# Recurrent mixer's head: transposed inputs and a first mix written tile by tile, in a fixed order on ScalarE and VectorE

## The chip, the cores and the metric

The kernel runs on one core of a Trainium2 chip. Its time is device microseconds of one execution. The engines are named as the profile names them: PE (TensorE, matmuls and transposes), ACT (ScalarE), DVE (VectorE), POOL (GpSimd) and SP (SyncE, which issues most DMAs).

## What is computed

A network of several layers in float32 on 256 tokens of width 1024. The change lies in one of them, the recurrent (RWKV) mixer of layer 2. Its reference, cut to what matters here:

```python
def rwkv7_time_mix(x, mu, w_rkv, w0, w1, w2, a0, a1, a2, g1, g2, ...):   # x is the normed input
    xx = jnp.pad(x, ((0, 0), (1, 0), (0, 0)))[:, :-1] - x        # previous token minus this one
    xr, xw, xk, xv, xa, xg = (x + xx * mu[i] for i in range(6))  # six mixes, indices 0 to 5
    r = xr @ w_rkv[0]
    k = xk @ w_rkv[1]
    v = xv @ w_rkv[2]
    w = -jax.nn.softplus(-(w0 + jnp.tanh(xw @ w1) @ w2)) - 0.5
    a = jax.nn.sigmoid((a0 + (xa @ a1) @ a2))
    g = jax.nn.sigmoid(xg @ g1) @ g2
    ...                                                          # then the recurrence over the tokens
```

The mixes have the indices r 0, w (the decay) 1, k 2, v 3, a 4, g 5.

## The kernel before

**Tiles.** The 256 tokens are two tiles of 128 (`TT`, t0 and t1). `h[t]` holds a tile's residual stream. A float32 product is made of three passes over numbers split into a high and a low part: `c.mm3` issues lines 116 to 118 (high weights by high input, low weights by high input, high weights by low input). So every input of a projection is wanted as a pair `xTh`, `xTl`, and every weight as `whi`, `wlo`, which ACT (line 81) and DVE (line 82) make from the loaded stage `st`.

**The head.** `c.rstd` takes the sum of squares of a tile on ACT (`junk`, line 128), and POOL makes the factor `rpre` of it. ACT scales the tile by it into `un`, in two halves (line 765); PE transposes each half in four blocks into `pt` (line 767); DVE multiplies by the norm's gain into `uT` (line 768), copies the token ahead of the tile into column 0 (line 771), and takes `xx` as one difference of 128x1024 (line 775).

**The mixes.** `shifted(i)` makes mix i for both tiles, in halves of 4 blocks: four times `xg` = `xx` by `mu[i]` on ACT (line 794, 128x128 each), plus `uT` on DVE (line 795), the high part on ACT (line 796), the low part on DVE (line 797). `proj(i, j, store)` calls it for its own index i and multiplies by `w_rkv[j]`; `lora(i, w, n)` does the same for a narrow weight. The calls stand in this order:

```python
    proj(2, 1, k)
    proj(0, 0, r)
    middle(0, 1, w1, AF.Tanh)      # calls lora(1, w1, 64)
    middle(1, 4, a1, AF.Copy)      # calls lora(4, a1, 64)
    gate_middle()                  # calls lora(5, g1, 160)
    ...
    part1(0)
    proj(3, 2, v)
    part2(0)
    part1(1)
```

`part1` makes the decayed keys and rates of one half of the heads (lines 865 to 928: `th`, `pb`, `E`, `kn`, `ar`, `bk`, `L`); `part2` inverts small blocks in a long chain of short DVE instructions on `Tc` (lines 940 to 945), which reads `comp`, a block that has gone to DRAM and back; `merges` (from line 957) follows.

**What sets the order.** A scheduler lays the instructions of the program on the five engines' queues by a simulated timeline; each queue then runs in its order, and waits are semaphores. So an edit at one place can move instructions that come much later.

Of the kernel before, what the change touches and what calls it, by code (L numbers as in the profile page):

```python
# [8 lines left out]
F32 = mybir.dt.float32  # L9
# [3 lines left out]
AF = mybir.ActivationFunctionType  # L13
# [3 lines left out]
D = 1024  # L17
# [634 lines left out]
def rwkv(c, pre, *args):  # L652
    with c.pool("rwkv") as mix, ExitStack() as phases:
        return rwkv_body(c, mix, pre, phases, *args)
# [58 lines left out]
def rwkv_body(c, mix, pre, phases, h, gpre, gpost, w_rkv, w0, w1, w2, a0, a1, a2, g1, g2, k_k, k_a, r_k, lnx_g,  # L713
              lnx_b, w_o):
    nc = c.nc
    HF = range(2)
    A = phases.enter_context(c.pool("rwkvA"))
    pad(A, 704)
    front = ExitStack()
    P1 = front.enter_context(c.pool("rwkvP"))  # L720
    close_A = phases.close
    open_B = lambda: phases.enter_context(c.pool("rwkvB"))
    TT = range(2)
    gb = c.load_bcast(gpost, "gb")
    muT, cum, mL, mK, mB, lowm, upm = pre.muT, pre.cum, pre.mL, pre.mK, pre.mB, pre.lowm, pre.upm
# [25 lines left out]
    def ring(shape, name):  # L751

        turn[0] ^= 1
        return c.wp.tile(shape, F32, name=name, tag="whi" if turn[0] else "wlo")

    ahead = {(1, 0): c.wblock(w_rkv[1], 0, 8, 0, 512)}

    uT, xx = [], []
    for t in TT:
        r = c.rstd(h[t], D, 1e-6, name="rpre")  # L760
        u = A.tile([128, 8, 129], F32, name=f"uT{t}")
        for q in range(2):
            pt = c.psT.tile([128, 4, 128], F32, name="pt", tag="pt")
            un = P1.tile([128, 512], F32, name="un", bufs=2)
            nc.scalar.activation(un, h[t][:, q * 512:q * 512 + 512], AF.Copy, scale=r)
            for k in range(4):
                nc.tensor.transpose(pt[:, k, :], un[:, k * 128:(k + 1) * 128], c.ident)
            nc.vector.tensor_mul(u[:, 4 * q:4 * q + 4, 1:], pt,
                                 gpre[:, 4 * q:4 * q + 4].unsqueeze(2).to_broadcast([128, 4, 128]))
        if t:  # L770
            nc.vector.tensor_copy(u[:, :, 0:1], uT[0][:, :, 128:129])
        else:
            nc.vector.memset(u[:, :, 0:1], 0.0)
        x = ring([128, 8, 128], f"xx{t}")
        nc.vector.tensor_sub(x, u[:, :, :128], u[:, :, 1:])
        uT.append(u)
        xx.append(x)

    nth = [0]

    def shifted(i):

        out = []
        for q in range(2):
            nth[0] += 1
            pool = P1 if i != 3 and nth[0] % 3 == 0 else c.act
            out.append([pool.tile([128, 4, 256], F32R, name="xT" + e, tag="xT" + e) for e in "hl"])
        for t in TT:
            s = slice(t * 128, t * 128 + 128)
            for q, (hi, lo) in enumerate(out):  # L790
                x = c.work.tile([128, 4, 128], F32, name="xg", tag="xg")
                for k in range(4):
                    kk = 4 * q + k
                    nc.scalar.activation(x[:, k], xx[t][:, kk], AF.Copy, scale=muT[:, kk, i:i + 1])
                nc.vector.tensor_add(x, x, uT[t][:, 4 * q:4 * q + 4, 1:])
                nc.scalar.copy(hi[:, :, s], x)
                nc.vector.tensor_sub(lo[:, :, s], x, hi[:, :, s])
        return out

    def lora(i, w, n):  # L800

        ws = c.wblock(w, 0, 8, 0, n)
        xs = shifted(i)
        G = c.psG.tile([128, 2, 256], F32, name="G", tag="G")
        m = lambda o, l, r, **kw: nc.tensor.matmul(o, l, r, skip_group_check=True, **kw)
        for e, c0 in enumerate(range(0, n, 128)):
            c1 = min(n, c0 + 128)
            o = G[:c1 - c0, e]
            for k in range(8):
                (wh, wl), (xh, xl) = ws(k), xs[k // 4]  # L810
                m(o, wh[:, c0:c1], xh[:, k % 4], start=(k == 0 and e == 0), stop=False)
                m(o, wl[:, c0:c1], xh[:, k % 4], start=False, stop=False)
                m(o, wh[:, c0:c1], xl[:, k % 4], start=False, stop=(k == 7 and c1 == n))
        return G
# [18 lines left out]
    r, k, v = {}, {}, {}  # L833

    def proj(i, j, store):
        xs = shifted(i)
        for q in HF:
            ws = ahead.pop((j, q), None) or c.wblock(w_rkv[j], 0, 8, q * 512, 512)
            for t in TT:
                G = c.psG.tile([128, 512], F32, name="G", tag="G")  # L840
                for kk in range(8):
                    xh, xl = (x[:, kk % 4, t * 128:t * 128 + 128] for x in xs[kk // 4])
                    c.mm3(G, xh, xl, *ws(kk), kk == 0, kk == 7)
                store[t, q] = S2(f"rkv{j}{t}{q}", f"rkv{j}", 4)
                nc.scalar.copy(store[t, q], G)  # L845
# [146 lines left out]
    def part3(q):  # L992
# [7 lines left out]
        for t in TT:  # L1000
# [91 lines left out]
            y[t, q] = yc  # L1092

    proj(2, 1, k)
    proj(0, 0, r)
    middle(0, 1, w1, AF.Tanh)
    middle(1, 4, a1, AF.Copy)
    gate_middle()
    front.close()
    phase[0] = phases.enter_context(c.pool("rwkvA2"))  # L1100
# [4 lines that stand above are left out]
# [738 lines left out]
```

## Time and profile before

| | us |
|---|---|
| median of 3 runs | 3363.42 |
| lowest and highest | 3344.17 and 3366.97 |
| the profiled execution | 3360.23 |
| its span in the trace | 3358.4 |
| busy: PE, DVE, ACT, POOL | 3185.8, 2342.0, 1595.5, 160.7 |
| mean granted clock of PE | 0.972 |

The span is the time from the first to the last instruction of one execution; the profiled execution's own time is 1.83 us longer. Busy times are sums over the whole span, so a stage in which PE waits is to be looked for in the windows and timelines. A matmul's end is modelled, so that durations of matmuls in a row overlap; the distance between their starts is the pace.

### The profile page before, as it was taken

How to read it: one execution, taken by the hardware profiler on the slowest of the kernel's cores; microseconds unless marked ns; L12 is line 12 of the kernel's file. 1: busy time of each engine (PE TensorE's matmuls, PEld its weight loads, DVE VectorE, ACT ScalarE, POOL GpSimd, SP SyncE). 2: the span in 40 equal slices, each digit the busy share in tenths (PEclk: the TensorE clock that was granted, in tenths of full speed). 3: DMA queues.
4: the chain of work that ended last, by engine and by line, in shares of the span. 5: the costliest groups of instructions: out<-in, count | busy, mean ns of one | idle time of the engine just before them, and what ended most of it. 6: DMA issues, size and time to landing. Idle time of an engine off the chain costs nothing. (4 is left out here: it accounts for less than half of the span.)

```text
span 3358.4 us, 45240 instructions
## 1 busy us (share of the span) xinstructions
PE 3185.8 (95%) x16491; PEld 2615.0 (78%) x16491; DVE 2342.0 (70%) x3767; ACT 1595.5 (48%) x2734; POOL 160.7 (5%) x248
## 2 busy tenths in 40 slices
PE   8999999989999987899999999999999999999898
PEld 7877887877887766787878877887778887775797
DVE  6767767777767766656777676765579877637787
ACT  5455454555445456224454465545544334424453
POOL 0001000000000001001010001010000000011000
PEclk9999999999999998889999999999999999998899
DMA  7663657643765753414656645631027554431463
GB/s 240 214 200 98 219 179 228 214 144 102 232 212 188 233 163 95 131 34 138 219 182 222 198 135 192 216 121 49 13 70 228 172 159 138 142 107 40 151 184 99
DMA packets 424667, 529.12 MB, mean 158 GB/s; under 512 B 54982, under 2 KB 342792, under 8 KB 424444
## 3 DMA queue, kind: packets, MB, share of 16 engines
q1 hardware_dynamic: 399548, 519.15, 49.4%
q10 hardware_dynamic: 24896, 7.08, 0.9%
q8 instruction: 130, 2.13, 0.3%
q14 instruction: 93, 0.76, 0.1%
HBM read 520.35 MB, written 5.78 MB: 157 GB/s over the span
## 5 line engine op out<-in xcount | busy, mean ns | idle before, releaser
L82 DVE TENSOR_TENSOR wlo<-st,whi 128x1024 fp32r<-128x1024 f32 (+1 forms) x810 | 974.4, 1215 | 406.6 <-ACT whi L81 370.2
L81 ACT CAST whi<-st 128x1024 fp32r<-128x1024 f32 (+1 forms) x810 | 835.7, 1044 | 533.5 <-PE po L118 173.1
L118 PE MATMUL G<-whi,xTl 128*128 128x512 f32 x1792 | 709.4, 396 | 19.2 <-DVE xTl L183 19.0
L116 PE MATMUL G<-whi,xTh 128*128 128x512 f32 x1792 | 714.6, 399 | 9.2 <-ACT rkv L845 2.2
L117 PE MATMUL G<-wlo,xTh 128*128 128x512 f32 x1792 | 705.9, 394 | 3.8 <-DVE wlo L79 3.8
L118 PEld LDWEIGHTS G<-whi,xTl 128*128 128x128 f32 x1792 | 338.8, 189 | 96.6 <-DVE xTl L183 27.0
L116 PEld LDWEIGHTS G<-whi,xTh 128*128 128x128 f32 x1792 | 339.3, 189 | 78.7 <-ACT whi L81 2.8
L117 PEld LDWEIGHTS G<-wlo,xTh 128*128 128x128 f32 x1792 | 339.3, 189 | 72.6 <-DVE wlo L79 5.7
L116 PE MATMUL po<-whi,hh 128*128 128x512 f32 x968 | 379.6, 392 | 9.1 <-ACT hh L260 7.2
L117 PE MATMUL po<-wlo,hh 128*128 128x512 f32 x968 | 377.6, 390 | 0.0
L118 PE MATMUL po<-whi,hl 128*128 128x512 f32 x968 | 339.9, 392 | 1.0 <-DVE hl L1743 0.5
L1707 PE MATMUL G<-xh,whi 128*128 128x256 f32 (+1 forms) x720 | 243.8, 339 | 8.4 <-ACT ub L1711 4.9
L1708 PE MATMUL G<-xl,whi 128*128 128x256 f32 (+1 forms) x720 | 242.1, 336 | 1.1 <-DVE xl L1232 1.1
L1709 PE MATMUL G<-xh,wlo 128*128 128x256 f32 (+1 forms) x720 | 241.5, 336 | 0.0
L251 ACT ACTIVATE sg<-G,rpre 128x256 f32<-128x256 f32 x176 | 83.8, 476 | 292.5 <-PE G L118 289.1
L116 PEld LDWEIGHTS po<-whi,hh 128*128 128x128 f32 x968 | 181.8, 188 | 50.6 <-ACT hh L260 10.9
L118 PEld LDWEIGHTS po<-whi,hl 128*128 128x128 f32 x968 | 180.5, 188 | 40.2 <-DVE hl L261 2.0
L1175 DVE SCALAR_TENSOR_TENSOR aa<-aw,sc,aa 128x1024 f32<-128x1024 f32 x140 | 174.9, 1282 | 51.5 <-DMA aw<-in_ada_w_dram 51.4
L117 PEld LDWEIGHTS po<-wlo,hh 128*128 128x128 f32 x968 | 181.8, 188 | 37.2
L1707 PEld LDWEIGHTS G<-xh,whi 128*128 128x128 f32 x720 | 138.8, 193 | 22.8 <-ACT ub L1711 5.3
L1708 PEld LDWEIGHTS G<-xl,whi 128*128 128x128 f32 x720 | 139.1, 193 | 15.4 <-DVE xl L1232 1.5
L1709 PEld LDWEIGHTS G<-xh,wlo 128*128 128x128 f32 x720 | 138.9, 193 | 14.3
(483 smaller groups left out, 4336.5 us busy)
## 6 DMA issues: line engine op xcount, KB each, us to landing
st<-in_ffn_w_in_dram SPq DMA_DIRECT2D x704, 256.0 KB, 4.1
st<-in_ffn_w_out_dram SPq DMA_DIRECT2D x242, 512.0 KB, 4.1
aw<-in_ada_w_dram SPq DMA_DIRECT2D x96, 512.0 KB, 4.7
st<-in_ffn_w_in_dram SPq DMA_DIRECT2D x88, 512.0 KB, 4.6
st<-in_swa_w_qkv_dram SPq DMA_DIRECT2D x24, 512.0 KB, 4.8
st<-in_gla_w_in_dram SPq DMA_DIRECT2D x24, 512.0 KB, 4.5
st<-in_rwkv_w_rkv_dram SPq DMA_DIRECT2D x24, 512.0 KB, 4.5
st<-in_na_w_qkv_dram SPq DMA_DIRECT2D x24, 512.0 KB, 4.1
```

Of the source, the lines that this page charges most:

```text
L81: nc.scalar.copy(hi, st)
L82: nc.vector.tensor_sub(lo, st, hi)
L116: m(out, xh, wh, start=start, stop=False)
L117: m(out, xh, wl, start=False, stop=False)
L118: return m(out, xl, wh, start=False, stop=stop)
L251: nc.scalar.activation(sg, G[:, :256], AF.Tanh, scale=rs[t][1])
L1175: nc.vector.scalar_tensor_tensor(acc[s], st, x, acc[s], op0=OP.mult, op1=OP.add)
L1707: m(Gf[:, a:b], wh, xh[:, k, a:b], start=(k == 0 and a == 0), stop=False, **kw)
L1708: m(Gf[:, a:b], wh, xl[:, k, a:b], start=False, stop=False, **kw)
L1709: m(Gf[:, a:b], wl, xh[:, k, a:b], start=False, stop=(k == 7 and b == ns * 256), **kw)
```

## The change

`shifted` is cut in two: `halves(i)` takes the buffers, `shift(i, t, out)` computes one tile's mix. The head is then one loop over the two tiles, inside a block in which ACT and DVE keep the written order of the block's own instructions (the scheduler may still set others between them). Per tile it is: sum of squares and `rpre`, column 0, both halves of `un`, then half by half the transposes, `uT`, and a difference `xx` of 128x512 (it was one of 128x1024 behind both halves); then `shift(1, t, mixed[1])` for the same tile. The mix so made is kept in `mixed` under the index 1, and `proj` asks `mixed` for its own index before it calls `shifted`.

```diff
-    uT, xx = [], []
-    for t in TT:
-        r = c.rstd(h[t], D, 1e-6, name="rpre")
...
-            un = P1.tile([128, 512], F32, name="un", bufs=2)
-            nc.scalar.activation(un, h[t][:, q * 512:q * 512 + 512], AF.Copy, scale=r)
...
-        x = ring([128, 8, 128], f"xx{t}")
-        nc.vector.tensor_sub(x, u[:, :, :128], u[:, :, 1:])
...
-    def shifted(i):
+    def halves(i):
...
+    def shift(i, t, out):
+        s = slice(t * 128, t * 128 + 128)
+        for q, (hi, lo) in enumerate(out):
+            x = c.work.tile([128, 4, 128], F32, name="xg", tag="xg")
+            for k in range(4):
+                kk = 4 * q + k
+                nc.scalar.activation(x[:, k], xx[t][:, kk], AF.Copy, scale=muT[:, kk, i:i + 1])
+            nc.vector.tensor_add(x, x, uT[t][:, 4 * q:4 * q + 4, 1:])
+            nc.scalar.copy(hi[:, :, s], x)
+            nc.vector.tensor_sub(lo[:, :, s], x, hi[:, :, s])
+
+    def shifted(i):
+        out = halves(i)
...
+    uT, xx = [], []
+    mixed = {1: halves(1)}
+    with c.tc.manual_schedule(engines={mybir.EngineType.Activation, mybir.EngineType.DVE}):
+        for t in TT:
+            r = c.rstd(h[t], D, 1e-6, name="rpre")
...
+            for q, un in enumerate(uns):
...
+                nc.vector.tensor_mul(u[:, z, 1:], pt, gpre[:, z].unsqueeze(2).to_broadcast([128, 4, 128]))
+                nc.vector.tensor_sub(x[:, z], u[:, z, :128], u[:, z, 1:])
+            uT.append(u)
+            xx.append(x)
+            shift(1, t, mixed[1])
...
     def proj(i, j, store):
-        xs = shifted(i)
+        xs = mixed.pop(i, None) or shifted(i)
```

The edit moves all later lines down by 13 (818 is the narrow product, 858 the copy of a projection, 880 and 957 are 867 and 944 of before). In the rows below a number behind a name tells one buffer from the next; `x4` is four instructions alike.

ACT at the head, from the second tile's sum of squares on, before:

```order
L128 ACTIVATE junk_11002,rprem_11001<-h1_91 128x1024
L794 ACTIVATE xg_11036<-xx0_10999,muT_10096 128x128 x4
L794 ACTIVATE xg_11044<-xx0_10999,muT_10096 128x128 x4
L765 ACTIVATE un_11009<-h1_91,rpre_11004 128x512
L765 ACTIVATE un_11017<-h1_91,rpre_11004 128x512
L796 CAST xTh_11032<-xg_11036 128x4x128
L796 CAST xTh_11034<-xg_11044 128x4x128
```

The same place now:

```order
L774 ACTIVATE xg_11008<-xx0_10993,muT_10096 128x128 x4
L776 CAST xTh_10975<-xg_11008 128x4x128
L774 ACTIVATE xg_11016<-xx0_10993,muT_10096 128x128 x4
L776 CAST xTh_10977<-xg_11016 128x4x128
L128 ACTIVATE junk_11025,rprem_11024<-h1_91 128x1024
L799 ACTIVATE un_11032<-h1_91,rpre_11027 128x512
L799 ACTIVATE un_11034<-h1_91,rpre_11027 128x512
L774 ACTIVATE xg_11051<-xx1_11036,muT_10096 128x128 x4
L776 CAST xTh_10975<-xg_11051 128x4x128
L774 ACTIVATE xg_11059<-xx1_11036,muT_10096 128x128 x4
L774 ACTIVATE xg_11077<-xx0_10993,muT_10096 128x128 x4
L776 CAST xTh_10977<-xg_11059 128x4x128
```

Both halves of the mix with index 1 (`xTh_10975`, `xTh_10977`) stand ahead of the second tile's sum of squares for t0 and behind its `un` for t1, and the first `xg` of the next mix (11077) comes behind them.

DVE behind the first tile's difference, before:

```order
L795 TENSOR_TENSOR xg_11036<-xg_11036,uT0_10981 128x512
L795 TENSOR_TENSOR xg_11044<-xg_11044,uT0_10981 128x512
L768 TENSOR_TENSOR uT1_11007<-pt_11008,gT_95 128x4x128
L797 TENSOR_TENSOR xTl_11033<-xg_11036,xTh_11032 128x4x128
L797 TENSOR_TENSOR xTl_11035<-xg_11044,xTh_11034 128x4x128
L768 TENSOR_TENSOR uT1_11007<-pt_11016,gT_95 128x4x128
L775 TENSOR_TENSOR xx1_11025<-uT1_11007 128x1024
L82 TENSOR_TENSOR wlo_11125<-st_11122,whi_11124 128x1024
L82 TENSOR_TENSOR wlo_11131<-st_11128,whi_11130 128x1024
L82 TENSOR_TENSOR wlo_11137<-st_11134,whi_11136 128x1024
```

And now, from the first half of the second tile's difference on:

```order
L808 TENSOR_TENSOR xx1_11036<-uT1_11030 128x512
L82 TENSOR_TENSOR wlo_11166<-st_11163,whi_11165 128x1024
L807 TENSOR_TENSOR uT1_11030<-pt_11044,gT_95 128x4x128
L82 TENSOR_TENSOR wlo_11172<-st_11169,whi_11171 128x1024
L82 TENSOR_TENSOR wlo_11178<-st_11175,whi_11177 128x1024
L808 TENSOR_TENSOR xx1_11036<-uT1_11030 128x512
L775 TENSOR_TENSOR xg_11051<-xg_11051,uT1_11030 128x512
L777 TENSOR_TENSOR xTl_10976<-xg_11051,xTh_10975 128x4x128
L775 TENSOR_TENSOR xg_11059<-xg_11059,uT1_11030 128x512
L775 TENSOR_TENSOR xg_11077<-xg_11077,uT0_10987 128x512
L777 TENSOR_TENSOR xTl_10978<-xg_11059,xTh_10977 128x4x128
L777 TENSOR_TENSOR xTl_11074<-xg_11077,xTh_11073 128x4x128
```

The second tile's difference is in halves with three `wlo` around the second transposed half, and the add into `xg_11077` stands behind both adds of the mix with index 1.

PE, the last transposes and the first products of the layer, before:

```order
L767 MATMUL pt_10990<-ident_85,un_10991 128x128 x4
L767 MATMUL pt_11008<-ident_85,un_11009 128x128 x4
L767 MATMUL pt_11016<-ident_85,un_11017 128x128 x4
L116 MATMUL G_11068<-whi_10953,xTh_11032 128x512
L117 MATMUL G_11068<-wlo_10954,xTh_11032 128x512
```

And now:

```order
L805 MATMUL pt_11001<-ident_85,un_10991 128x128 x4
L805 MATMUL pt_11037<-ident_85,un_11032 128x128 x4
L805 MATMUL pt_11044<-ident_85,un_11034 128x128 x4
L116 MATMUL G_11109<-whi_10953,xTh_11073 128x512
L117 MATMUL G_11109<-wlo_10954,xTh_11073 128x512
```

The order is the same; the product's inputs are now `xTh_11073` and `xTl_11074`, which stand on ACT and DVE behind the pairs 10975 to 10978 of the mix with index 1.

DVE late in the layer, where the last weight parts of the v projection (`wlo`, line 82) meet the chain of `part2(0)`, before:

```order
L82 TENSOR_TENSOR wlo_11940<-st_11937,whi_11939 128x1024
L904 TENSOR_TENSOR bo_12099<-rkv001_11363,km_12086 128x512
L902 SCALAR_TENSOR_TENSOR tha_12084<-tha_12084,kn_12089 128x512
L82 TENSOR_TENSOR wlo_11946<-st_11943,whi_11945 128x1024
L943 TENSOR_TENSOR pr_12005<-Tc_12003,comp_11646 128x1
L905 TENSOR_TENSOR bo_12099<-bo_12099,rkb_12060 128x512
L882 COPY em01_12080<-E1_12068 128x4
L944 TENSOR_REDUCE Tc_12003<-pr_12005 128x1
L907 TENSOR_REDUCE bon01_12102<-bo_12099 128x8
L943 TENSOR_TENSOR pr_12005<-Tc_12003,comp_11646 128x2x2
L944 TENSOR_REDUCE Tc_12003<-pr_12005 128x2
L943 TENSOR_TENSOR pr_12005<-Tc_12003,comp_11646 128x3x3
```

And now:

```order
L957 TENSOR_REDUCE Tc_12044<-pr_12046 128x3
L956 TENSOR_TENSOR pr_12046<-Tc_12044,comp_11687 128x4x4
L957 TENSOR_REDUCE Tc_12044<-pr_12046 128x4
L956 TENSOR_TENSOR pr_12046<-Tc_12044,comp_11687 128x5x5
L957 TENSOR_REDUCE Tc_12044<-pr_12046 128x5
L956 TENSOR_TENSOR pr_12046<-Tc_12044,comp_11687 128x6x6
L957 TENSOR_REDUCE Tc_12044<-pr_12046 128x6
L956 TENSOR_TENSOR pr_12046<-Tc_12044,comp_11687 128x7x7
L82 TENSOR_TENSOR wlo_11981<-st_11978,whi_11980 128x1024
L957 TENSOR_REDUCE Tc_12044<-pr_12046 128x7
L82 TENSOR_TENSOR wlo_11987<-st_11984,whi_11986 128x1024
L956 TENSOR_TENSOR pr_12046<-Tc_12044,comp_11687 128x8x8
```

The last two `wlo` of that projection (11940 and 11946) stood ahead of the chain's first step; they (11981 and 11987) now stand behind the product and the sum of its seventh step.

## Rows read from the trace of the kernel before

**Rows 1.** The page, part 1: busy us and share of each engine.

```profile
PE 3185.8 (95%) x16491; PEld 2615.0 (78%) x16491; DVE 2342.0 (70%) x3767; ACT 1595.5 (48%) x2734; POOL 160.7 (5%) x248
```

**Rows 2.** Windows of the recurrent layer: length, busy us per engine, clock, DMA.

```profile
1221.50:1234.40 12.90, 3.13 (x18) 2.50 (x17) 9.02 (x17) 11.48 (x23) 2.50 (x6) 0.64 0.45 123
1234.40:1238.60 4.20, 4.20 (x12) 3.13 (x11) 4.17 (x6) 0.83 (x3) 0.00 (x0) 0.50 0.00 0
1238.60:1276.50 37.90, 37.70 (x166) 30.74 (x165) 27.30 (x33) 29.85 (x65) 0.00 (x0) 1.00 0.60 183
1276.50:1310.00 33.50, 22.27 (x128) 18.00 (x126) 21.88 (x37) 26.90 (x75) 4.56 (x2) 0.85 0.05 18
1310.00:1382.50 72.50, 56.80 (x260) 43.73 (x260) 52.99 (x104) 18.93 (x33) 6.10 (x6) 0.78 0.51 145
```

**Rows 3.** PE's timeline at the head: start, duration, work, [idle before].

```profile
1224.16 1.46 PE L767 MATMUL pt<-ident,un 128*128 128x128 f32 x8 [2.61 <-ACT un L765]
1232.77 1.97 PE L767 MATMUL pt<-ident,un 128*128 128x128 f32 x8 [7.16 <-ACT un L765]
1234.39 0.78 PE L116 MATMUL G<-whi,xTh 128*128 128x512 f32 x1
...
1242.39 0.50 PE L116 MATMUL G<-whi,xTh 128*128 128x512 f32 x1 [0.20 <-ACT xTh L796]
```

**Rows 4.** Timeline of ACT over the same stretch.

```profile
1223.38 1.34 ACT L765 ACTIVATE un<-h,rpre 128x512 f32<-128x512 f32 x2 [0.41 <-POOL rpre L147]
1224.62 2.92 ACT L81 CAST whi<-st 128x1024 fp32r<-128x1024 f32 x3
1228.22 1.06 ACT L128 ACTIVATE junk<-h 128x1024 bf16<-128x1024 f32 x1 [0.67 <-DVE h L301]
...
1229.66 2.44 ACT L794 ACTIVATE xg<-xx,muT 128x128 f32<-128x128 f32 x8 [0.29 <-DVE xx L775]
1232.01 1.32 ACT L765 ACTIVATE un<-h,rpre 128x512 f32<-128x512 f32 x2
1233.23 1.12 ACT L796 CAST xTh<-xg 128x512 fp32r<-128x512 f32 x2
```

**Rows 5.** Timeline of DVE over the same stretch.

```profile
1228.41 1.22 DVE L775 TENSOR_TENSOR xx<-uT 128x1024 f32<-128x1024 f32 x1
...
1230.97 0.69 DVE L795 TENSOR_TENSOR xg<-xg,uT 128x512 f32<-128x512 f32 x1 [1.26 <-ACT xg L794]
...
1233.92 0.69 DVE L768 TENSOR_TENSOR uT<-pt,gT 128x512 f32<-128x512 f32 x1 [1.09 <-PE pt L767]
1234.53 1.28 DVE L797 TENSOR_TENSOR xTl<-xg,xTh 128x512 fp32r<-128x512 f32 x2
...
1237.59 3.49 DVE L82 TENSOR_TENSOR wlo<-st,whi 128x1024 fp32r<-128x1024 f32 x3
```

**Rows 6.** Timeline of POOL over the same stretch.

```profile
1229.83 0.57 POOL L147 TENSOR_TENSOR rpre<-rprem,mhalf 128x1 f32<-128x1 f32 x1
```

**Rows 7.** Line 794: all of them, and what ACT waited for.

```profile
L794 ACT ACTIVATE xg<-xx,muT x96: 384/388/404, 1229.7 to 1305.6; 128x128 f32<-128x128 f32 x96
...
  DVE xTl L797: 2.3, 4
```

**Rows 8.** Timelines late in the layer: ACT, then DVE, then PE.

```profile
1369.33 2.44 ACTq L742 DMA_DIRECT2D Ld<-L  x1
1371.82 0.60 ACT L867 ACTIVATE th<-z 128x512 f32<-128x512 f32 x1 [8.71 <-DMA g2b<-in_rwkv_g_dram]
...
1349.88 0.16 DVE L943 TENSOR_TENSOR pr<-Tc,comp 128x1 f32<-128x1 f32 x1 [1.78 <-DMA comp<-Ld]
...
1352.95 0.20 DVE L943 TENSOR_TENSOR pr<-Tc,comp 128x36 f32<-128x36 f32 x1
...
1373.02 2.06 PE L876 MATMUL pb<-cum,th 128*128 128x129 f32 x8 [5.47 <-DVE th L869]
...
1382.56 1.86 PE L957 MATMUL ps<-Z,L 128*128 128x128 f32 x7
```

More of the change, by code (lines that the diff above doesn't have):

```diff
@@ L756, in rwkv_body @@
     ahead = {(1, 0): c.wblock(w_rkv[1], 0, 8, 0, 512)}
-    uT, xx = [], []
-    for t in TT:
-        r = c.rstd(h[t], D, 1e-6, name="rpre")
-        u = A.tile([128, 8, 129], F32, name=f"uT{t}")
-        for q in range(2):
-            pt = c.psT.tile([128, 4, 128], F32, name="pt", tag="pt")
-            un = P1.tile([128, 512], F32, name="un", bufs=2)
-            nc.scalar.activation(un, h[t][:, q * 512:q * 512 + 512], AF.Copy, scale=r)
[L766 to L773, printed above, removed]
-        x = ring([128, 8, 128], f"xx{t}")
-        nc.vector.tensor_sub(x, u[:, :, :128], u[:, :, 1:])
-        uT.append(u)
-        xx.append(x)
     nth = [0]
-    def shifted(i):
+    def halves(i):
         out = []
@@ L787, in shifted @@
             out.append([pool.tile([128, 4, 256], F32R, name="xT" + e, tag="xT" + e) for e in "hl"])
-        for t in TT:
-            s = slice(t * 128, t * 128 + 128)
-            for q, (hi, lo) in enumerate(out):
-                x = c.work.tile([128, 4, 128], F32, name="xg", tag="xg")
-                for k in range(4):
[L793 to L797, printed above, removed]
@@ L798, in shifted @@
-        return out
+        return out
+    def shift(i, t, out):
[8 more added lines that the diff above has]
+            nc.vector.tensor_sub(lo[:, :, s], x, hi[:, :, s])
@@ new lines, in shifted @@
+    def shifted(i):
+        out = halves(i)
+        for t in TT:
+            shift(i, t, out)
+        return out
+    uT, xx = [], []
[3 more added lines that the diff above has]
+            r = c.rstd(h[t], D, 1e-6, name="rpre")
+            u = A.tile([128, 8, 129], F32, name=f"uT{t}")
+            if t:
+                nc.vector.tensor_copy(u[:, :, 0:1], uT[0][:, :, 128:129])
+            else:
+                nc.vector.memset(u[:, :, 0:1], 0.0)
+            uns = []
+            for q in range(2):
+                un = P1.tile([128, 512], F32, name="un", bufs=2)
+                nc.scalar.activation(un, h[t][:, q * 512:q * 512 + 512], AF.Copy, scale=r)
+                uns.append(un)
+            x = ring([128, 8, 128], f"xx{t}")
+            for q, un in enumerate(uns):
+                pt = c.psT.tile([128, 4, 128], F32, name="pt", tag="pt")
+                for k in range(4):
+                    nc.tensor.transpose(pt[:, k, :], un[:, k * 128:(k + 1) * 128], c.ident)
+                z = slice(4 * q, 4 * q + 4)
+                nc.vector.tensor_mul(u[:, z, 1:], pt, gpre[:, z].unsqueeze(2).to_broadcast([128, 4, 128]))
[3 more added lines that the diff above has]
+            shift(1, t, mixed[1])
```

## The prediction

> **What bounds the kernel now.** I read the page's engine shares first: PE is busy for 95% of the span [rows 1], so an edit pays only where PE stands still. The windows of this layer come next. While the head runs, PE works 3.13 of 12.90 us and ACT 11.48 [rows 2]; in the projections behind it PE is full (37.70 of 37.90 us); then come two stages in which PE idles again (22.27 of 33.50 and 56.80 of 72.50 us). The head's timelines say what ends the 12.90 us. PE's first product starts at 1234.39, behind the transposes of tile t1 at 1232.77, which had waited 7.16 us for ACT's `un` [rows 3]. ACT runs `un` of t0, three weight casts to 1227.54, t1's sum of squares, the eight `xg` of t0 at 1229.66 and `un` of t1 at 1232.01, then the two casts that the first product needs [rows 4]. DVE is always a step behind or ahead of that [rows 5]. So the head is one serial path through ACT, DVE and PE, and whatever is put into it shifts a stretch in which PE has no slack.
>
> **What the change does, read from the code.** It makes a first mix in the head and keeps it under index 1, the decay. `proj` asks for its own index, and its calls are 2, 0 and 3; index 1 is wanted only by `lora`, which calls `shifted(1)` and never asks. So nobody reads the new mix. The order shows it: PE's first product reads `xTh_11073` and `xTl_11074`, which belong to the mix of index 2, and the pairs 10975 to 10978 have no reader. The change therefore adds a whole mix to the serial path: 16 `xg` and 4 casts on ACT, 4 adds and 4 subtractions on DVE. That is 16 x 0.293 (the pace of eight `xg` in 2.44 us, one lasting 0.388 [rows 4, 7]) + 4 x 0.51 (the pace of two casts in 1.12) = 6.7 us of ACT and 8 x 0.59 (the pace of two in 1.28 [rows 5]) = 4.7 us of DVE.
>
> **The head, step by step.** I replay the queues of the order with the durations of the rows, on the clock of the trace before; nothing changes up to the casts that end at 1227.54.
>
> - t0. In halves, the first difference stands one DVE slot of 0.59 earlier than the whole one at 1228.41, so it runs 1227.82 to 1228.51, and `xg` starts at 1228.54 instead of 1229.66. The unread mix then runs step by step, since ACT's cast waits for DVE's add: four `xg` to 1229.81 (3 x 0.293 + 0.388), add to 1230.55, cast to 1231.2; the second half's `xg` to 1232.36, add to 1233.09, cast to 1233.74.
> - Only then comes t1's sum of squares, at 1233.63. From it to `rpre` it took 2.18 us (1228.22 to 1230.40 [rows 4, 6]), so `un` of t1 starts at 1235.84 instead of 1232.01: 3.8 us later. From `un` to `uT` it took 1.91 (1232.01 to 1233.92 [rows 4, 5]): 1237.75.
> - t1's differences. Between the first `uT` and the second half of `xx` stand, on DVE, one half of `xx`, another `uT` and three `wlo` of 1.14 each (3.49 for three): 3 x 0.60 + 3 x 1.14 = 5.2 us, so that the last half of `xx` starts at 1243.0 and ends at 1243.7. The unread mix's add for t1 stands behind it by the written order, though its `xg` is done at 1240.5; ACT stands for nearly 4 us. Add to 1244.35, cast to 1245.0, the second half's `xg` to 1246.1.
> - The mix that is read. Four `xg` to 1247.3, add to 1248.05, cast to 1248.7, and there the first product starts: **14.3 us later** than 1234.39. The wait of 0.20 inside the projections [rows 3] goes, since the weights' parts are long made: 14.1.
>
> Bounds: the unread work cannot cost less than ACT's 6.7 us less the 1.42 that ACT idles in that window [rows 2], so 5.3; add four hand-overs between ACT and DVE at up to 0.4 more than I allow, and it is 16. The transposes gain nothing; their cover is gone anyway, since PE is idle on both sides of them. [...]
>
> The halving of `xx` has a small price of its own. By the rows two halves at a pace of 0.59 to 0.60 take 0.07 to 0.1 us more than one of 1.22 [rows 5]. [...]
>
> **Behind the head.** In the projections and the narrow products every engine's work is the same and keeps its neighbours, so it shifts as a whole. Two places are re-ordered by the scheduler. In front of `part1(0)` the gate's activation now stands ahead of `th`, on which PE waits: 1 us, between 0 and 2. Late, the last two `wlo` of the v projection stand behind the seventh step of the chain on `Tc`. That chain starts when `comp` lands (1349.88) and was at its sixth step at 1352.95 [rows 8]; so the weights come some 7 us after PE could use them, of which about 2 are won back because PE starts that stretch earlier: 5 us, all of which I pass on to the merges at 1382.56 [rows 8]. The bounds are 0, if the later wait of PE for `th` (5.47) takes it up, and 12: the last copy of v and an `E` now stand on ACT behind the DMA issues of `part2(0)`, and such a queue held `th` for 8.71 us there [rows 8]. What follows the layer is re-ordered a little, at nothing or up to 2 us either way.
>
> Sum: 14.1 + 1 + 5 = 20 us. On the profiled execution's 3360.23 that is 3380.3; the median of the runs before is 3.2 higher, which would give 3383.5. I take **3382**.
>
> **The rivals.**
>
> 1. *The mix does what the edit says, or hides.* If the unread work could be passed over, only t1's late `un` would stay: the first product at about 1238.2, +3.8, and 3366 with the rest of the sum not spent. Against it: ACT is busy 11.48 of 12.90 us in that window [rows 2]. ACT would have to run a ready `xg` of the read mix ahead of a waiting cast; where `th` waited 8.71 us, it did so behind the queue's DMA issues [rows 8]. [...] A toolchain that drops writes nobody reads would give about the same time. 6 in 100.
> 2. *The late re-ordering costs nothing.* PE's wait for `th` takes it up: 3360.2 + 15 = 3375, some 3378 by the median. 16 in 100.
> 3. *Faster after all.* In the two stages behind the projections PE idles 11.23 and 15.70 us [rows 2]. With PE 14 us late, weights, mixes and DMAs are further ahead of it, and those waits could shrink. The price: to win, they must give back over 20 of 26.9 us, and the time would be about 3355. It decides whether they wait for stock or for a chain. Only 2.3 us of ACT's waits for `xTl` are of the first kind [rows 7]; the 5.47 us before `pb` end with DVE's `th`, which follows ACT and PE of the same stage [rows 8]. 4 in 100 for any gain, 2 for one of over 1%.
> 4. *Clearly slower.* The chain's wait for `comp` and the DMA issues on ACT add up: +12 at the second place instead of +5, with the head at its upper bound: 3360.2 + 16 + 2 + 12 = 3390, 3393 by the median; a further slip of t1's `th` by a queue like the 8.71 us puts it at 3400. It decides whether the last `wlo` are late by more than the 10 us or so that the merges are away. 14 in 100, some 9 of them beyond 1%.
>
> **How the numbers follow.** The forecast has 60 in 100: 3374 to 3390. About 1%, 33.6 us, is what a measurement of this kernel can tell from no change (three runs before lie within 22.8 us), so the forecast, a loss of 0.6%, falls within it. The range takes in rival 2 and the better part of rivals 1 and 4: 3360 to 3401. Faster by over 1%: 0.02; within 1%: 0.88; slower by over 1%: 0.10.
>
> **What would show it.** In the trace of the changed kernel: 112 `xg` instead of 96; PE's idle time ahead of the first product some 14 us longer, ended by the cast of line 776, with t1's transposes near 1236.6; ACT standing about 4 us ahead of a cast at 1244; the window of the projections as long as before; and PE waiting some 7 us in the v projection for `wlo` of line 82. I am wrong if the first product starts before 1240 (rival 1), or if the head is as replayed but the merges start less than 10 us later (rivals 2 and 3) or more than 28 (rival 4).

## The result

The changed kernel took 3389.84 us (median of six runs, 3380.38 to 3411.25), the kernel before 3353.42 in the same comparison (six runs, among them the three of the table ahead of the prediction): a ratio of 1.0106, with an interval of 1.0084 to 1.0128. Timed a second time (run e5 below) it was 1.0070, 1.0047 to 1.0094. It is slower by 20 to 36 us; the forecast was 20, and 3382. The profiled execution took 3385.51 us with a span of 3383.7.

The page's engine shares (busy us, share, instructions), against [rows 1], show 20 more instructions on ACT and 10 more on DVE; PE has as many as before and is busy 15.8 us longer. The group of line 774 shows where most of ACT's come from, 16 more `xg` than the 96 of before [rows 7]; the other four are casts:

```profile
PE 3201.6 (95%) x16491; PEld 2620.5 (77%) x16491; DVE 2343.8 (69%) x3777; ACT 1605.4 (47%) x2754; POOL 154.7 (5%) x248
```

and, in the group's row:

```profile
L774 ACT ACTIVATE xg<-xx,muT x112: 384/387/404, 1231.4 to 1324.4; 128x128 f32<-128x128 f32 x112
```

The windows of the stages (length, busy us with instruction counts, granted clock, DMA; cut where PE's starts lie, so that they do not fall on the borders of [rows 2]): the head has grown from 13.23 to 28.19 us between PE's starts, and PE works 4.12 us in it; the projections behind it are full as before.

```profile
1223.40:1251.60 28.20, 4.12 (x18) 2.70 (x16) 19.41 (x31) 17.48 (x41) 2.44 (x6) 0.56 0.39 112
1251.60:1298.10 46.50, 46.47 (x192) 38.10 (x193) 28.62 (x37) 35.76 (x80) 0.00 (x0) 0.93 0.41 126
1298.10:1324.00 25.90, 18.64 (x102) 15.39 (x100) 16.15 (x27) 21.07 (x60) 0.00 (x0) 0.80 0.01 4
1324.00:1406.10 82.10, 62.22 (x268) 46.60 (x268) 57.47 (x111) 21.88 (x42) 8.70 (x8) 0.74 0.47 128
```

PE's timeline at the head, against [rows 3] (start, duration, work, idle time before it and what ended it): the transposes of t1 wait 11.27 us instead of 7.16, and behind them PE stands for another 10.23, ended by the cast of the first mix that anybody reads.

```profile
1226.44 1.73 PE L805 MATMUL pt<-ident,un 128*128 128x128 f32 x8 [2.61 <-ACT un L799]
1239.43 1.97 PE L805 MATMUL pt<-ident,un 128*128 128x128 f32 x8 [11.27 <-ACT un L799]
1251.63 0.79 PE L116 MATMUL G<-whi,xTh 128*128 128x512 f32 x1 [10.23 <-ACT xTh L776]
```

ACT's timeline, against [rows 4]. The first two `xg` groups, with the casts behind them, are the unread mix of t0. Only then come t1's sum of squares (1236.52) and `un` (1238.66). The unread `xg` of t1 (1242.04) is followed by 3.93 us in which ACT stands.

```profile
1225.67 1.33 ACT L799 ACTIVATE un<-h,rpre 128x512 f32<-128x512 f32 x2 [0.42 <-POOL rpre L147]
...
1231.40 1.28 ACT L774 ACTIVATE xg<-xx,muT 128x128 f32<-128x128 f32 x4 [1.57 <-DVE xx L808]
1233.44 0.62 ACT L776 CAST xTh<-xg 128x512 fp32r<-128x512 f32 x1 [0.76 <-DVE xg L775]
1233.96 1.27 ACT L774 ACTIVATE xg<-xx,muT 128x128 f32<-128x128 f32 x4
...
1236.52 1.05 ACT L128 ACTIVATE junk<-h 128x1024 bf16<-128x1024 f32 x1
...
1238.66 1.33 ACT L799 ACTIVATE un<-h,rpre 128x512 f32<-128x512 f32 x2 [0.99 <-POOL rpre L147]
1242.04 1.28 ACT L774 ACTIVATE xg<-xx,muT 128x128 f32<-128x128 f32 x4 [2.05 <-DVE xx L808]
1247.24 0.62 ACT L776 CAST xTh<-xg 128x512 fp32r<-128x512 f32 x1 [3.93 <-DVE xg L775]
...
1250.96 0.62 ACT L776 CAST xTh<-xg 128x512 fp32r<-128x512 f32 x1 [0.25 <-DVE xg L775]
```

DVE over the same stretch, against [rows 5], shows what it stands for: the second half of t1's difference (line 808, 1245.92) comes behind the three `wlo`, two of them in one row here, and the add that ACT waits for (line 775) behind that. `kab` at the top waits 0.53 us for its own load, and the first difference behind it.

```profile
1230.34 0.43 DVE L872 TENSOR_SCALAR kab<-kab 128x512 f32<-128x512 f32 x1 [0.53 <-DMA kab<-in_rwkv_k_a_dram]
1230.68 0.69 DVE L808 TENSOR_TENSOR xx<-uT 128x512 f32<-128x512 f32 x1
...
1243.65 2.35 DVE L82 TENSOR_TENSOR wlo<-st,whi 128x1024 fp32r<-128x1024 f32 x2
1245.92 0.68 DVE L808 TENSOR_TENSOR xx<-uT 128x512 f32<-128x512 f32 x1
1246.52 0.68 DVE L775 TENSOR_TENSOR xg<-xg,uT 128x512 f32<-128x512 f32 x1
```

### The profile page after: what moved, and what is told of

Same layout as the page of the kernel before. It is cut to its first block, busy times and chain, and to the rows that moved or that the text cites. A ratio compares the mean times of both kernels' runs of the same rounds, so it can differ in the third digit from the quotient of the medians.

```text
span 3383.7 us, 45274 instructions
## 1 busy us (share of the span) xinstructions
PE 3201.6 (95%) x16491; PEld 2620.5 (77%) x16491; DVE 2343.8 (69%) x3777; ACT 1605.4 (47%) x2754; POOL 154.7 (5%) x248
```

## The experiments

All times of stages are distances between starts in PE's timeline of each profiled run: from the last product of the layer before to the first product of this one ("head"), to the first narrow product, to the first `pb`, to the first merge. Ratios are to the kernel before, timed beside each.

| run | head | to narrow | to pb | to merges | sum | ratio (interval) |
|---|---|---|---|---|---|---|
| before | 13.23 | 46.26 | 21.83 | 80.08 | 161.4 | |
| changed | 28.19 | 46.50 | 25.87 | 82.11 | 182.7 | 1.0106 (1.0084 to 1.0128) |
| e5 changed again | 27.58 | 45.22 | 24.63 | 84.97 | 182.4 | 1.0070 (1.0047 to 1.0094) |
| e1 no first mix | 12.56 | 46.33 | 21.74 | 84.17 | 164.8 | 1.0011 (0.9994 to 1.0029) |
| e2 index 2 | 10.47 | 57.98 | 21.79 | 86.48 | 176.7 | 1.0027 (1.0010 to 1.0044) |
| e3 unread mix in before | 25.06 | 46.56 | 25.56 | 77.06 | 174.2 | 1.0028 (1.0013 to 1.0043) |
| e4 interleaved | 10.84 | 49.99 | 20.49 | 79.39 | 160.7 | 1.0007 (0.9989 to 1.0025) |
| e6 rotation kept | 28.02 | 46.47 | 23.71 | 84.18 | 182.4 | 1.0053 (1.0031 to 1.0075) |
| e7 unread mix later | 12.23 | 54.97 | 21.69 | 84.42 | 173.3 | 1.0035 (1.0019 to 1.0052) |
| e8 interleaved, held | 10.23 | 50.57 | 22.25 | 76.83 | 159.9 | 1.0004 (0.9987 to 1.0022) |
| e9 late order back | 28.23 | 45.43 | 24.68 | 75.22 | 173.6 | 1.0056 (1.0036 to 1.0077) |
| e10 no written order | 23.99 | 45.49 | 24.71 | 81.19 | 175.4 | 1.0078 (1.0060 to 1.0095) |
| e11 halves only | 12.84 | 47.17 | 22.48 | 78.10 | 160.6 | 0.9978 (0.9963 to 0.9993) |
| e12 the same again | 12.96 | 45.79 | 23.29 | 78.34 | 160.4 | 1.0001 (0.9982 to 1.0020) |

**e1: the changed kernel without the first mix.**

```diff
-    mixed = {1: halves(1)}
+    mixed = {}
...
-            shift(1, t, mixed[1])
```

> The changed kernel without the first mix in the head; the halves of the differences and the written order stay. Theory (the unread mix is the cost): from the last product of the layer before to the first product of this layer 13 us within 1.5, as before (13.2) and not 28.2 as in the changed kernel; the late re-ordering of the weights stays, so the time is 0 to 6 us over the kernel before, ratio 1.000 to 1.003. Rival (the written order is the cost): over 20 us there, ratio 1.006 or more.

Head 12.56, ratio 1.0011: halves and written order together, without the mix, cost nothing there, they even gain 0.7 us. The late stretch is longer though (84.17 against 80.08), as the order said it would be. PE's timeline of this run, the last transposes (behind them the products follow at once):

```profile
1232.74 1.97 PE L805 MATMUL pt<-ident,un 128*128 128x128 f32 x8 [6.67 <-ACT un L799]
1234.36 0.78 PE L116 MATMUL G<-whi,xTh 128*128 128x512 f32 x1
```

**e2: the mix kept under the index that is asked for.**

```diff
-    mixed = {1: halves(1)}
+    mixed = {2: halves(2)}
...
-            shift(1, t, mixed[1])
+            shift(2, t, mixed[2])
```

> The changed kernel with the mix kept under index 2, which the first projection asks for, so that it is read. Theory: ACT does the same work up to the casts of tile t0, but PE now wants them: the first product comes about 10 us behind the last one of the layer before (3 us sooner than in the kernel before), and t1's products, behind its transposes, about 1 us later than before; ratio to before 0.998 to 1.004. Rival (the written order, which puts the second tile behind the first tile's mix, is the cost): as slow as the changed kernel, 1.008 or more.

The first product comes 10.47 us behind the last one, as the replay of this order said, but the ratio is still 1.0027, and the layer 15.3 us longer. The scheduler now puts t1's transposes behind the 24 products of t0, and PE's timeline shows the price, a wait of 6.93 us for t1's mix:

```profile
1233.10 0.79 PE L116 MATMUL G<-whi,xTh 128*128 128x512 f32 x1 [5.50 <-ACT xTh L776]
...
1241.56 1.03 PE L805 MATMUL pt<-ident,un 128*128 128x128 f32 x8
1249.53 0.80 PE L116 MATMUL G<-whi,xTh 128*128 128x512 f32 x1 [6.93 <-ACT xTh L776]
```

I had expected t1's products one us late; they came 5.7 us late (26.90 us behind the last product of the layer before instead of 21.23), since the place of the transposes and the three `wlo` in front of t1's second half were left out of that sum.

**e3: the kernel before with an unread mix.**

```diff
     def proj(i, j, store):
+        if i == 2:
+            shifted(1)
         xs = shifted(i)
```

> The kernel before with one extra mix of index 1 that nobody reads, ahead of the first projection's own; no written order, whole differences. It adds work and leaves nothing out. Theory: the first product about 24.5 us behind the last one of the layer before (11.5 more than before, since t1's scaled input isn't held up), and some 4 us more in the narrow products, whose buffers rotate otherwise; the late weights keep their place; ratio 1.004 to 1.006. Rival (written order): 13 us and ratio 1.000 to 1.002.

The head grew by 11.83 us with no written order at all, forecast 11.5. So the extra work alone is most of the cost; what the changed kernel has beyond it, 2.5 to 3.1 us in the head, e10 takes apart. PE's timeline of it:

```profile
1240.58 1.97 PE L767 MATMUL pt<-ident,un 128*128 128x128 f32 x8 [7.25 <-ACT un L765]
1253.91 0.80 PE L116 MATMUL G<-whi,xTh 128*128 128x512 f32 x1 [11.35 <-ACT xTh L796]
```

ACT's timeline says why 6.7 us of ACT's work cost 11.8. The first two rows are the kernel before, t1's part of the mix that is read: ACT waits 3.41 us for t1's `xx` and 1.49 for the add that stands behind three `wlo` on DVE, but PE has t0's products meanwhile. The other two are e3: the unread mix has the same two waits, and now they stand in front of PE's first product. 6.7 of work and 4.9 of waits make 11.6.

```profile
1237.77 2.45 ACT L794 ACTIVATE xg<-xx,muT 128x128 f32<-128x128 f32 x8 [3.41 <-DVE xx L775]
1241.72 0.62 ACT L796 CAST xTh<-xg 128x512 fp32r<-128x512 f32 x1 [1.49 <-DVE xg L795]
...
1245.58 2.45 ACT L794 ACTIVATE xg<-xx,muT 128x128 f32<-128x128 f32 x8 [3.41 <-DVE xx L775]
1249.53 1.22 ACT L796 CAST xTh<-xg 128x512 fp32r<-128x512 f32 x2 [1.50 <-DVE xg L795]
```

**e4: both tiles interleaved.** Index 2, and the second half of the block in this order (`scaled` makes the two `un`; `turned` does the transposes, `uT` and the difference of a half):

```diff
+        shift_half(2, 0, 0, *mixed[2][0])
+        uns = scaled(1, r)
+        shift_half(2, 0, 1, *mixed[2][1])
+        for q, un in enumerate(uns):
+            turned(1, q, un)
+            shift_half(2, 1, q, *mixed[2][q])
```

> Index 2, and the second tile's sum of squares and scaled input written between the halves of the first tile's mix, so that neither tile waits for the whole of the other. Theory: first product 9 to 11 us behind the last one of the layer before, t1's products 1 to 3 us sooner than in the kernel before, nothing moved in the late stage: 0 to 5 us under the kernel before, ratio 0.998 to 1.000. Rival (written order costs by itself): over the kernel before by 0.3% or more.

Head 10.84, but the projections take 3.7 us more, and the time can't be told from before (1.0007).

**e5: the changed kernel again.**

> The changed kernel once more, as a control, since the first comparison had six runs a side. If the layer is what the change costs, the stretch from the last product of the layer before to the merges is again 21 us longer than before (182.7 against 161.4), and the ratio 1.006 to 1.008, below the first 1.011; if the change also slows stretches outside the layer, 1.010 or more.

182.4 against 182.7: the layer's loss repeats within 0.3 us, though the stages in it differ by up to 2.9 us, while the ratio fell from 1.0106 to 1.0070, into the range that the layer explains.

**e6: the buffers of the later mixes as before.**

```diff
     mixed = {1: halves(1)}
+    nth[0] = 0
```

> The changed kernel with the counter that rotates the mixes' buffers set back behind the unread mix, so that the later mixes lie in the pools of before. Head unchanged: 28.2 us to the first product. Theory A (the narrow products' extra 4 us come of the rotation): 22 to 23 us from the first narrow product to the first pb, as before (21.8). Theory B (they come of an order that the scheduler moved: the second waT activation ahead of a cast that PE wants; the order still has it here): 24 to 26, the activation of the gate being back behind th.

23.71 us to `pb`, between what the two theories gave, so this run doesn't settle it: the gate's activation went back behind `th` with the buffers, and 1 to 2 of the 3 to 4 us with it, while PE's wait of 2.24 us in front of the third group of narrow products stayed as in the changed kernel, with the order that sets it. The clock granted here was 0.78, in the changed kernel's two profiles 0.80 and 0.86, so the 2 us against the first of them are the better measure. The changed kernel's rows for that place, ACT and then PE: the cast of line 776 stands behind the `waT` activation of line 836, which waits for PE.

```profile
1309.52 0.38 ACT L836 ACTIVATE waT<-G 64x256 f32<-64x256 f32 x1 [1.43 <-PE G L818]
1309.80 0.60 ACT L776 CAST xTh<-xg 128x512 fp32r<-128x512 f32 x1
...
1309.95 1.12 PE L898 MATMUL z<-a2e,waT 65*128 65x512 f32 x2 [0.47 <-ACT waT L836]
1313.31 0.58 PE L818 MATMUL G<-xTh,whi 128*128 128x256 f32 x1 [2.24 <-ACT xTh L776]
```

**e7: the unread mix behind the first projection.** On top of the edit of e1:

```diff
     proj(2, 1, k)
+    held = nth[0]
+    shifted(1)
+    nth[0] = held
     proj(0, 0, r)
```

> The unread mix is moved out of the head, behind the first projection, where ACT has idle time; the head is that of the kernel without a mix, and no work is left out against the changed kernel. Theory (it costs because it is in front of the first product): 12.6 us to the first product, 46 to 47 in the projections, and no more than 4 us in all over the kernel without the mix; ratio to before 1.000 to 1.003. Rival (extra work costs wherever it stands): projections 6 us longer or more, ratio 1.004 or more.

The rival was right in the stage: the head is short (12.23), but the projections are 8.7 us longer than before; the ratio, 1.0035, lies between the two. ACT's spare time there was not enough: in the kernel before it stood still for 1.33 of the 15.16 us between t1's first cast and about the start of the second projection (1242.24 to 1257.40). In e7 it is busy for 22.05 of 23.50 us (1242.55 to 1266.05), and the second projection's mix is late, as PE's timeline shows.

```profile
1243.71 0.50 PE L116 MATMUL G<-whi,xTh 128*128 128x512 f32 x1 [1.19 <-ACT xTh L776]
...
1266.05 0.79 PE L116 MATMUL G<-whi,xTh 128*128 128x512 f32 x1 [5.73 <-ACT xTh L776]
```

**e8: interleaved, with the weights held back.** On top of e4, t1's first half is turned ahead of t0's second mix half, the `wlo` of the first projection and `kab` wait behind the head's last subtraction:

```diff
-        nc.vector.tensor_sub(lo, st, hi)
...
+            with self.tc.issue_after(self.behind.ins):
+                nc.vector.tensor_sub(lo, st, hi)
```

> As the interleaved version with index 2, and t1's first transposed half is turned ahead of t0's second mix half; the weights' low parts and the scaling of kab wait behind the head's last subtraction. Theory (t1's mix was late by the three wlo between its halves): first product 10 to 11 us behind the last one of the layer before, first product to first narrow one 47 to 48.5 instead of 50.0; the layer 2 to 4 us shorter than before; ratio 0.997 to 1.001. Rival (the wlo are then late for the second half of the columns): a wait of over 1 us on wlo and no gain.

No gain: PE waits 1.97 us for t1's second cast half, which now stands behind a weight cast and four `xg` of the next mix on ACT. The layer is 1.5 us shorter than before, the ratio 1.0004.

**e9: the late order put back.** In `part2(0)` the first step of the chain stands behind the last `wlo` of the v projection:

```diff
+            first = c.tc.issue_after(c.last_lo.ins) if i == 1 and q == 0 else ExitStack()
+            with first:
+                nc.vector.tensor_mul(pr[:, :i, :i], Tc[:, :i, :i], ...)
```

> The changed kernel with only the chain of the first inversion held behind the last low part of the v projection's weights, as in the kernel before. Theory (the late re-ordering costs what was forecast, 5 us): head unchanged at 27.5 to 28.3, from the first pb to the merges 77 to 80 us instead of 82 to 85; ratio 1.004 to 1.008. Rival (that stretch varies by the clock or by DMAs and not by this order): 82 to 85 again.

75.22 us from `pb` to the merges instead of 82.11 and 84.97: that order is the cause. Holding the chain moved more than one row: PE no longer waits for a `wlo`, and the last v copy and `E` come ahead of the last four of `part2(0)`'s six DMA issues on ACT, so that PE waits 2.67 us for `E` instead of 7.42. The two together are 6.4 of the 6.9 us against the first profile. ACT, then PE:

```profile
1380.98 0.58 ACT L858 COPY rkv<-G 128x512 f32<-128x512 f32 x1 [6.48 <-DVE kn L906]
...
1382.18 1.12 PE L932 MATMUL pt<-ident,rkv 128*128 128x128 f32 x4 [2.67 <-ACT E L892]
```

The ratio, 1.0056, is lower than the changed kernel's by 0.50% and 0.14%; 7 to 10 of 3360 us would be 0.2 to 0.3%. Its interval overlaps with that of e5, so the ratios alone don't settle it; the stage does.

**e10: the changed kernel without the written order.**

```diff
-    with c.tc.manual_schedule(engines={mybir.EngineType.Activation, mybir.EngineType.DVE}):
+    if True:
```

> The changed kernel with its unread mix and its halves, but without the fixed order on ACT and DVE. Theory (the unread mix costs 11 to 12, the written order 3 more, since it puts t1's sum of squares behind t0's unread mix): 24.5 to 25.5 us to the first product instead of 27.6 to 28.2; late stretch as in the changed kernel; ratio 1.004 to 1.008. Rival (the written order is the larger part): under 20 us.

Head 23.99: with the unread mix in place, the written order is 3.6 to 4.2 of the head's 14 to 15 us, the unread mix the other 11. Without the mix it cost nothing (e1), so it costs by what it puts t1 behind: `un` of t1 comes 8.22 us behind that of t0 here and 12.99 in the changed kernel. The late re-ordering is there in e1, without the mix, and here, without the written order, so neither alone brings it about; it is missing in e3, e4 and e8, and what in the edit moves it, no run separates.

**e11 and e12: the best of the parts.** The edits of e1 and e9 together, run twice.

> Halves and written order without any first mix, and the inversion's chain held behind the v projection's weights. Theory: 12.3 to 12.8 us to the first product, 0.7 under the kernel before, and 77 to 80 in the late stretch; so the layer is 0 to 2 us shorter than before and the ratio 0.998 to 1.001: too little to be told from no change. Rival (the late stretch does not depend on that order): 84 there and ratio 1.001 or more.

> The kernel of the run before once more, since it was the only one timed faster than the kernel before (0.9978) while its layer was only 0.8 us shorter in the trace. If the gain is real and lies in the layer, the ratio is again 0.996 to 0.999; if it was luck of the granted clock in the stretches behind the layer, 0.999 to 1.002. To the first product 12.3 to 12.9 us, in the late stretch 77 to 80.

The first time it was faster than before by 0.2%, the second time not at all (1.0001), with the same stages in the trace. The layer is 0.8 to 1.0 us shorter; the rest of the first gain was not in it. The interval of one comparison doesn't cover what differs from one comparison to the next, here as with the changed kernel and e5. No version here is shown to beat the kernel before.

## Why the prediction came out right, point by point

- **The unread mix and the head: right.** Forecast 14.3 us, measured 14.96 and 14.35, and the first product, at 1251.63, excludes rival 1 as the prediction put it (before 1240). The steps hold: `un` of t1 12.99 us behind that of t0 instead of 8.63 [rows 4], 4.4 later where I said 3.8 (half a us of it is `kab`'s wait for its load, which the order put ahead of the first difference and I priced as work only); ACT's stand 3.93 where I said nearly 4, while the `xg` of the read mix for t0, whose `xx` was done at 1232.69, stood further back in its queue, the second four of the eight from 1247.77. The split was not asked for, but e3 and e10 give it: about 11 us the work with its waits, about 4 the place of t1's sum of squares behind it.
- **The halves: the sign was off.** I took 0.07 to 0.1 us of loss from the rows; without the unread mix the head is 0.3 to 1.0 us shorter (e1, e7, e11, e12). These runs have the written order too, so the gain is not that of the halves alone. In e10, without it, the first `xg` starts without the 0.29 us that it waited for the whole `xx`, and `un` of t1 comes 8.22 us behind that of t0 instead of 8.63; in e1 it comes 7.95 behind, and t1's sum of squares no longer waits 0.67 us for `h`.
- **"It shifts as a whole": the projections yes, the narrow products no.** The projections took 46.50 and 45.22 us instead of 46.26, at granted clocks of 0.93, 0.96 and 0.95. In the narrow products the changed kernel lost 4.0 and 2.8 us; I had looked at the rows in front of `part1(0)` and not at the second `waT` activation, which the scheduler moved ahead of a cast that PE wants. It moves the third group of products by 1.7 us (3.36 from the `z` products to it, 1.68 before). The gate's activation ahead of `th`, forecast 1 us, gave a wait of 1.97 instead of 1.30 ahead of `pb` and took 0.9 off the next one: nothing in sum. These two, 1.7 and 0.7, are most of the 2.8. The 1.2 us between the two profiles are the clock, 0.80 granted in the first and 0.86 in the second: the same 102 matmuls keep PE busy for 18.61 and 17.31 us.
- **The late re-ordering: the size right, the mechanism half.** Forecast 5 us; the two profiles of the changed kernel have 2.0 and 4.9 over the one of before. From `pb` to the merges the seven profiles with the new order (changed, e1, e2, e5, e6, e7, e10) have a mean of 83.9 us, the seven with the old one (in e3 and e4 with the last `wlo` behind the chain's first step) 77.9, and e9, e11 and e12 show the order as the cause: 6 us. But it is not the 7 us wait for `wlo` that I named. The changed kernel's rows, DVE, then ACT, then PE: both `wlo` were done at 1376.05, and PE waited 1.69 us for one; the longer wait, 7.42, is for `E`, which stood on ACT behind the last v copy (1389.91), and that behind the DMA issues of `part2(0)`. In all seven profiles with the new order PE waits 7.1 to 7.9 us for this `E`, and 0.4 to 1.7 for a `wlo`. That queue was the mechanism I kept for the upper bound and for the rival that was clearly slower: the term came out near its size with its price put on the wrong wait, and that is luck.

```profile
1373.55 1.22 DVE L82 TENSOR_TENSOR wlo<-st,whi 128x1024 fp32r<-128x1024 f32 x1
...
1374.83 1.22 DVE L82 TENSOR_TENSOR wlo<-st,whi 128x1024 fp32r<-128x1024 f32 x1
...
1386.64 3.23 ACTq L742 DMA_DIRECT2D Z<-Zd  x2
1389.91 0.59 ACT L858 COPY rkv<-G 128x512 f32<-128x512 f32 x1 [11.23 <-issue]
...
1374.82 0.50 PE L117 MATMUL G<-wlo,xTh 128*128 128x512 f32 x1 [1.69 <-DVE wlo L82]
...
1391.12 1.12 PE L932 MATMUL pt<-ident,rkv 128*128 128x128 f32 x4 [7.42 <-ACT E L892]
```

- **The total.** The layer lost 21.3 and 21.0 us, forecast 20. The sum is nearer than its terms: the narrow products lost 2 to 3 us more than forecast, and in the first profile the late stretch lost 3 less. The first comparison's further 15 us are not in the layer, and the second doesn't have them. By them the first median, 3389.84, lies at the very end of the forecast's 3374 to 3390, and its ratio, 1.0106, in the loss of over 1% that had 10 in 100, not in the band within 1% that had 88; the second, 1.0070, lies in that band. And 1% was not the least that can be told: an interval of 1.0047 to 1.0094 tells a loss of 0.7% from no change.
- **Rival 1 was priced wrongly.** With the right index the first product is not 3.8 us late but 2.8 early, since the scheduler then moves t1's transposes behind t0's products; the loss comes later, in t1 (e2). So the edit as it was probably meant is slower too, by 15 us in the layer. Rival 2 (the late order costs nothing) fell with e9. Rival 3 fell as a gain: in the changed kernel PE's two idle stages did not shrink with PE 15 us late. But they were re-ordered at the same time, and in the two runs with PE late and the late order of before, e3 and e9, the stretch from `pb` to the merges is 77.06 and 75.22 us against 76.83 to 80.08 in the five with PE on time; that such a stage gives a few us back is not excluded. Rival 4 (clearly slower) had the mechanism of the late stretch right and its price, 12 us, too high.

## What to carry to other kernels

A buffer made ahead and looked up by a key is worth one check in the order of the built program: who reads it. Extra work on a serial path cost more than its own length here, some 11 us for 6.7 us of ACT work: its waits for the other engine (3.41 and 1.50 us in e3), which other work had covered, came with it. Moved out of the path it cost 8.7 (e7), because the engine that looked idle there had less spare time up to the moment its next result was wanted (1.33 us in the kernel before) than the work needs. And an edit at the head of a layer can move the scheduler's order far behind it, here some 130 us and 130 DVE instructions later: that was a quarter of the loss, and holding one instruction gave it back.

## What was not expected of the hardware

The same stretch of dense products behind the merges ran at different granted clocks from run to run. Two windows in each kernel from the first merge on (100 us, then 40), the kernel before first, then e2. PE is busy for 38.54 of 40 us in the kernel before, as in the 100 us ahead of them (97.70), and the clock granted is 0.66 of full speed: 0.50 in 26 of the 40 single microseconds (1484.56 to 1497.56 and 1505.56 to 1518.56), 0.96 to 1.00 in the others but for two (0.70 and 0.72); in e2 the mean is 1.00.

```profile
1382.56:1482.56 100.00, 97.70 (x829) 87.02 (x828) 62.61 (x135) 27.76 (x44) 3.84 (x4) 0.97 0.24 68
1482.56:1522.56 40.00, 38.54 (x200) 32.13 (x199) 14.92 (x32) 4.97 (x9) 1.90 (x2) 0.66 0.09 27
```

```profile
1399.35:1499.35 100.00, 97.98 (x851) 87.60 (x850) 62.81 (x136) 28.35 (x46) 3.85 (x4) 1.00 0.25 68
1499.35:1539.35 40.00, 35.75 (x246) 29.59 (x246) 24.13 (x53) 7.35 (x15) 4.88 (x6) 1.00 0.09 27
```

From POOL's marks the kernel e2, 15 us late at the merges, is level with the kernel before some 150 us later, and e11 gains 7 us in the same place (e12 too, 6): the orders on the queues differ a little there too, and no run separates the two, but the clock is what the windows show. One kernel alone shows it as well: the first 100 us from the merges on in the two profiles of the changed kernel, with 832 and 767 matmuls done in them.

```profile
1406.11:1506.11 100.00, 98.08 (x832) 87.31 (x832) 62.62 (x135) 28.29 (x45) 3.85 (x4) 0.97 0.24 68
...
1404.60:1504.60 100.00, 97.23 (x767) 87.92 (x768) 58.32 (x126) 24.68 (x40) 3.84 (x4) 0.88 0.23 63
```

The stretch ahead of this layer, in which PE's products stand in the same order in every kernel, ended between 1221.08 and 1228.85 us in these profiles. And the executions of one kernel go with their mean granted clock: of e6's twelve the fastest, 3362.48 us, had 0.974, the slowest, 3399.70, had 0.964. That is the noise under the ratios here, and why the stages in the trace, which repeat within 1 us for the head, decide more than the medians do. What makes the clock fall at one time and not at another in a stretch that PE fills, no run here shows.
